# LayerNorm rows in PSUM, alternating half products and a fifth operand slot in a Strassen-type MLP

## The chip, the core and the metric

One core of a Trainium2 chip runs the whole kernel. The metric is the device time in microseconds, the median of several executions. The engines: PE (TensorE, matrix products into PSUM), DVE (VectorE), ACT (ScalarE), POOL (GpSimd), SP (SyncE, which issues most transfers). [...]

## The reference

A layer on 1024 tokens and 16 meta tokens, width 1024, fp32: LayerNorm, an input projection, three mixers (stick-breaking attention, a convolution module, a short gated convolution), an output projection, LayerNorm, an MLP and a last LayerNorm. The change touches the MLP's second product and the last LayerNorm:

```python
h = layer_norm(DEEPNORM_ALPHA * h + mix, ln_mix_g, ln_mix_b)
ff = jnp.square(jax.nn.relu(h @ w1)) @ w2       # 1024 -> 4096 -> 1024
h = layer_norm(DEEPNORM_ALPHA * h + ff, ln_ff_g, ln_ff_b)
return h[:, N_META:]
```

## The kernel before

Every fp32 matrix is split in a high part, rounded to the type that PE multiplies fast (`split`: ACT casts, DVE subtracts), and a low part; a product is three matmuls, high by high, high by low, low by high. The sum of all rows (1024 tokens x 1024 columns, eight row tiles of 128 tokens) stays in SBUF as `acc`.

The MLP runs in `NG` = 8 groups of 512 hidden columns (`ff_group`). First, four 128-column pieces of h @ w1 are formed for two halves of the tokens each (`ff1_chunk`); ACT applies relu out of PSUM, DVE squares into `ra`. Then the group's part of the second product is formed not by eight half products but by seven, of sums and differences of the quarters (a11 to a22 of the squares, b11 to b22 of w2), in the manner of Strassen and Winograd. The sums stand in `gsum` and run on POOL; `early_sums(1)` and the line behind it (L908 and L909) stand behind the last chunk of the first product. A `product` is, for each of four token tiles, 2 x 3 matmuls of 128x128 by 128x512 into one PSUM bank each; `add_to` adds the four banks to `acc` on DVE, and in the last group also writes each row's sum.

The operands of a half product are split by `a_part` (ACT casts, DVE forms the low part) and `b_part` (ACT casts, POOL forms the low part). Their parts lie in a ring of 4 slots of 8 KB per partition (L821): two for the product that runs, two for the next. PSUM has four banks with tag `g` for the products, three `t` and one `o` that are no longer used in the groups.

The scale and the offset of the last LayerNorm, `fg` and `fb`, are broadcast to SBUF before the groups (L960 to L963). In the last group `finish_rows` runs for a row tile as soon as its sums are complete, for tiles 0 to 3 after the fifth product, for tiles 4 to 7 after the last: the mean on POOL, the squares' sum on ACT (L870), the factor on POOL (L89, L91, L872), normalising on ACT (L873), scale on DVE (L874), offset on POOL, for the last tile on DVE (L876), output by SP (L877).

The order on each queue is set by a planner, which takes the program's order as priority and starts what it reckons to be ready; on the chip each engine then runs its queue in that fixed order. Waits for tiles and slots are put in by the same layer.

Of the kernel before, what the change touches and what calls it, by code (L numbers as in the profile page):

```python
# [8 lines left out]
F32 = mybir.dt.float32  # L9
F32R = mybir.dt.float32r  # L10
AF = mybir.ActivationFunctionType
ALU = mybir.AluOpType
# [3 lines left out]
P = 128  # L16
D = 1024
# [4 lines left out]
NT = S // P  # L22
# [13 lines left out]
def f32(ap):  # L36
    return ap.bitcast(F32)
# [3 lines left out]
def hybrid_layer(ctx: ExitStack, tc, x, meta_tokens, ln_in_g, ln_in_b, w_in, w_conf_dw, b_conf_dw,  # L41
                 ln_conf_g, ln_conf_b, w_short_dw, g_mix, w_out, ln_mix_g, ln_mix_b, w_ff1, w_ff2,
                 ln_ff_g, ln_ff_b, out):
    nc = tc.nc
    xs, os_ = x[0], out[0]
# [18 lines left out]
    def ps_t(shape):  # L64
        return ps.tile(shape, F32, tag="t", bufs=3, name="ps_t")

    def ps_o(shape):
        return ps.tile(shape, F32, tag="o", bufs=1, name="ps_o")
# [9 lines left out]
    first = cst.tile([P, 1], F32, name="first")  # L78
# [5 lines left out]
    def small(shape, name, bufs=4):  # L84
        return cst.tile(shape, F32, tag=name, bufs=bufs, name=name)

    def rsqrt(dst, src, n, w, scale, eps):
        ve = small([P, 8], "ve")
        nc.gpsimd.tensor_scalar(out=ve[:n, :w], in0=src, scalar1=scale, scalar2=eps,  # L89
                                op0=ALU.mult, op1=ALU.add)  # L90
        nc.gpsimd.tensor_tensor(out=dst, in0=ve[:n, :w], in1=mhalf[:n, :w], op=ALU.pow)  # L91
# [33 lines left out]
    def split(h, l, src):  # L125
        nc.scalar.copy(out=h, in_=src)  # L126
        nc.vector.tensor_tensor(out=l, in0=src, in1=f32(h), op=ALU.subtract)  # L127
# [5 lines left out]
    def raw_tile(name="raw"):  # L133
        return wA.tile([P, D], F32, tag="raw", bufs=2, name=name)
# [19 lines left out]
    def bcast_row(dst, row, eng=nc.scalar):  # L154
        eng.dma_start(out=dst, in_=row.partition_broadcast(P))
# [5 lines left out]
    rows = ph0.tile([P, 2, D], F32, name="rows")  # L161
# [628 lines left out]
    HALF = slice(0, 512), slice(512, 1024)  # L790
# [15 lines left out]
    def ff1_open(g, j):  # L806
        if j % 2 == 0:
            ra[j // 2] = wA.tile([P, 2, S], F32, tag="ff", bufs=2, name="relu2")
        u = 4 * g + (j + 2) % 4
        return halves(load_cols(w_ff1, u * P))  # L810

    def ff1(g, j):
        w = ff1_open(g, j)
        for c in range(2):
            ff1_chunk(j, w, c)

    def gsum(dst, a, b, op):
        nc.gpsimd.tensor_tensor(out=dst, in0=a, in1=b, op=op)  # L818

    def ring(name):  # L820
        return ffp.tile([P, 2, 2, 512], F32R, tag="ring", bufs=4, name=name)  # L821

    def a_part(src):
        hl = ring("a_hl")
        split(hl[:, 0], hl[:, 1], src)
        return hl

    def b_part(src):
        hl = ring("b_hl")
        nc.scalar.copy(out=hl[:, 0], in_=src)  # L830
        gsum(hl[:, 1], src, f32(hl[:, 0]), ALU.subtract)
        return hl

    def w2_load(g):

        rb = [ffp.tile([P, 2, D], F32, tag=f"w2_{h}", bufs=1, name=f"w2_{h}") for h in range(2)]
        for h in (1, 0):
            r0 = (4 * g + 2 * (1 - h)) * P
            nc.sync.dma_start(out=rb[h], in_=w_ff2[r0:r0 + 2 * P, :].rearrange("(u p) c -> p u c", p=P))
        return rb  # L840

    def product(a, b, banks, start):
        for tt in range(4):
            i = 0
            for u in range(2):
                for x, y in ((0, 0), (0, 1), (1, 0)):
                    nc.tensor.matmul(banks[tt], lhsT=a[:, x, u, tt * P:(tt + 1) * P], rhs=b[:, y, u, :],  # L847
                                     start=(start and i == 0), stop=(i == 5), skip_group_check=True)
                    i += 1

    def add_to(th, n, banks, first, sums=None):
        for tt in range(4):
            t = 4 * th + tt
            a = acc[:, t, HALF[n]]
            kw = {} if sums is None else dict(accum_out=sums[t][:, n:n + 1])
            if first:
                nc.vector.scalar_tensor_tensor(out=a, in0=a, scalar=ALPHA, in1=banks[tt], op0=ALU.mult, op1=ALU.add)
            elif sums is None:
                nc.vector.tensor_tensor(out=a, in0=banks[tt], in1=a, op=ALU.add)  # L859
            else:  # L860
                nc.vector.scalar_tensor_tensor(out=a, in0=banks[tt], scalar=1.0, in1=a, op0=ALU.mult, op1=ALU.add, **kw)

    def finish_rows(t, sm):

        a = acc[:, t, :]
        mv, rs = small([P, 2], "mv"), small([P, 2], "rs")
        nc.gpsimd.tensor_tensor(out=mv[:, 0:1], in0=sm[:, 0:1], in1=sm[:, 1:2], op=ALU.add)  # L867
        nc.gpsimd.tensor_scalar(out=mv[:, 1:2], in0=mv[:, 0:1], scalar1=-1.0 / D, scalar2=0.0, op0=ALU.mult, op1=ALU.add)  # L868
        junk = raw_tile("junk")
        nc.scalar.activation(out=junk, in_=a, func=AF.Square, bias=mv[:, 1:2], accum_out=sm[:, 2:3])  # L870
        rsqrt(rs[:, 0:1], sm[:, 2:3], P, 1, 1.0 / D, LN_EPS)
        nc.gpsimd.tensor_tensor(out=rs[:, 1:2], in0=rs[:, 0:1], in1=mv[:, 1:2], op=ALU.mult)  # L872
        nc.scalar.activation(out=a, in_=a, func=AF.Identity, scale=rs[:, 0:1], bias=rs[:, 1:2])  # L873
        nc.vector.tensor_tensor(out=a, in0=a, in1=fg, op=ALU.mult)  # L874
        eng = nc.vector if t == NT - 1 else nc.gpsimd
        eng.tensor_tensor(out=a, in0=a, in1=fb, op=ALU.add)  # L876
        nc.sync.dma_start(out=os_[t * P:(t + 1) * P, :], in_=a)  # L877

    def ff_group(g, opened=()):
        first, last = g == 0, g == NG - 1  # L880
        sums = {t: ffp.tile([P, 4], F32, tag="sums", bufs=NT, name="sums") for t in range(NT)} if last else None
        rb = w2_load(g)
        b11, b12 = (rb[0][:, :, h] for h in HALF)
        b21, b22 = (rb[1][:, :, h] for h in HALF)
        t1 = ffp.tile([P, 2, 512], F32, tag="t1", bufs=1, name="t1")
        gsum(t1, b12, b11, ALU.subtract)
        gsum(b12, b22, b12, ALU.subtract)
        for j in (2, 3, 0):
            if j not in opened:
                ff1(g, j)  # L890
        a11, a21 = (ra[0][:, :, h] for h in HALF)
        a12, a22 = (ra[1][:, :, h] for h in HALF)
        s1 = ffp.tile([P, 2, 512], F32, tag="s1", bufs=1, name="s1")

        def early_sums(u):
            gsum(s1[:, u], a21[:, u], a22[:, u], ALU.add)
            gsum(a21[:, u], a11[:, u], a21[:, u], ALU.subtract)

        early_sums(0)
        w = ff1_open(g, 1)  # L900
        ff1_chunk(1, w, 0)
        b, a = b_part(b21), a_part(a12)
        b_, a_ = b_part(b11), a_part(a11)
        gsum(b11, b22, t1, ALU.subtract)
        gsum(b21, b21, b11, ALU.subtract)
        gsum(a11[:, 0], s1[:, 0], a11[:, 0], ALU.subtract)
        ff1_chunk(1, w, 1)
        early_sums(1)  # L908
        gsum(a11[:, 1], s1[:, 1], a11[:, 1], ALU.subtract)  # L909

        def banks():
            return [ps_g([P, 512]) for _ in range(4)]

        pc = banks()
        product(a, b, pc, True)
        add_to(0, 0, pc, first)
        pa = banks()
        product(a_, b_, pa, True)
        add_to(0, 0, pa, False, sums)
        a, b = a_part(a11), b_part(b11)  # L920
        gsum(a12, a12, a11, ALU.subtract)
        product(a, b, pa, False)
        add_to(1, 0, pa, first)
        a, b = a_part(s1), b_part(t1)
        product(a, b, pa, False)
        add_to(1, 1, pa, first)
        a, b = a_part(a12), b_part(b22)
        product(a, b, pa, False)
        add_to(0, 1, pa, first, sums)
        if last:  # L930
            for t in range(4):
                finish_rows(t, sums[t])
        a, b = a_part(a21), b_part(b12)
        pb = banks()
        product(a, b, pb, True)
        add_to(1, 1, pb, False, sums)
        a, b = a_part(a22), b_part(b21)
        product(a, b, pb, False)
        add_to(1, 0, pb, False, sums)
        if last:  # L940
            for t in range(4, NT):
                finish_rows(t, sums[t])

    w0 = v_slot()
    raw = raw_tile()
# [1 line left out]
                      in_=w_ff1[:, 0:P].rearrange("(k p) c -> p k c", p=P))  # L947
# [9 lines left out]
    for pl in (attw, attq, keep):  # L957
        pl.release()
    ffp = pool("ffp", side="left")
    fg = ffp.tile([P, D], F32, name="fg")  # L960
    fb = ffp.tile([P, D], F32, name="fb")
    bcast_row(fg, ln_ff_g[0])
    bcast_row(fb, ln_ff_b[0])  # L963
    ff1_chunk(3, w1, 0)
    for g in range(NG):
        ff_group(g, (2, 3) if g == 0 else ())
# [28 lines left out]
```

## Time and profile before

| | |
|---|---|
| median of 3 runs | 1292.7 us (1291.52 to 1293.79) |
| profiled execution | 1289.94 us |
| its span in the trace | 1288.2 us |
| mean granted clock of PE | 0.968 |
| busy: PE, DVE, ACT, POOL | 1188.9, 861.4, 481.7, 432.5 us |
| last matmul starts | 1253.35 us |

The profile is that of one execution. A row of a timeline has the start in us from the span's start, the duration, the engine, the line of the kernel, the operation and its tiles, out<-in; in brackets the idle time of the engine before it and what ended it. PEld is PE's weight load. In tables of groups, the busy time is in us and the mean of one instruction in ns. Names of tiles are those of the program: `relu`, `s`, `w`, `t` are the operands ra, s1, w2 and t1.

### The profile page before, as it was taken

The numbers are of one execution on the slowest core, as the hardware profiler recorded it, in microseconds if no ns is written. First come the engines' busy times: TensorE is split into PE (matmuls) and PEld (weight loads), VectorE is DVE, ScalarE is ACT, GpSimd is POOL, SyncE is SP. The second block draws the span as 40 slices with busy tenths as digits, with TensorE's granted clock in tenths as the row PEclk, the third lists the DMA queues.
The fourth block names the chain that finished last, engine by engine and source line by source line (L and its number), as shares of the span: only waits on it lengthen the run. The fifth ranks groups of instructions, "written<-read, shape, count | busy, mean of one in ns | idle before, by whom it ended". The sixth has DMA issues, their size and how long they took to land. (4 is left out here: it accounts for less than half of the span.)

```text
span 1288.2 us, 15800 instructions
## 1 busy us (share of the span) xinstructions
PE 1188.9 (92%) x6126; PEld 1021.0 (79%) x6126; DVE 861.4 (67%) x1133; ACT 481.7 (37%) x883; POOL 432.5 (34%) x382
## 2 busy tenths in 40 slices
PE   5999996899899798989999999999999999999990
PEld 5999995889698687868778788887887878878870
DVE  6799967988787799674663645745447365463474
ACT  5422116667565554342322322322223222232243
POOL 3300002010100000240853634635436455353567
PEclk9999997999999899999999999999999999999995
DMA  9213211021201712103211111211211111111003
GB/s 296 108 50 82 65 35 50 17 50 34 50 18 41 221 34 66 50 17 109 72 66 33 33 66 49 64 35 49 66 50 46 53 49 66 37 30 66 1 2 129
DMA packets 71322, 78.97 MB, mean 61 GB/s; under 512 B 2329, under 2 KB 57920, under 8 KB 71248
## 3 DMA queue, kind: packets, MB, share of 16 engines
q1 hardware_dynamic: 66880, 67.18, 16.5%
q0 software_dynamic: 2304, 4.20, 1.7%
q10 hardware_dynamic: 2064, 6.59, 1.4%
q8 instruction: 48, 0.79, 0.3%
q14 instruction: 26, 0.21, 0.1%
HBM read 63.28 MB, written 10.49 MB: 57 GB/s over the span
## 5 line engine op out<-in xcount | busy, mean ns | idle before, releaser
L847 PE MATMUL ps_g<-b_hl,a_hl 128*128 128x512 f32 x1344 | 312.1, 392 | 6.3 <-POOL b_hl L818 3.8
L799 PE MATMUL ps_g<-x1h,w_hl 128*128 128x512 f32 x992 | 307.3, 389 | 0.0
L847 PEld LDWEIGHTS ps_g<-b_hl,a_hl 128*128 128x128 f32 x1344 | 252.6, 189 | 64.4 <-POOL b_hl L818 6.7
L208 PE MATMUL ps_g<-xh,w_hl 128*128 128x346 f32 (+4 forms) x1024 | 257.7, 331 | 0.9 <-ACT beta L458 0.9
L799 PEld LDWEIGHTS ps_g<-x1h,w_hl 128*128 128x128 f32 x992 | 186.2, 188 | 38.4
L818 POOL TENSOR_TENSOR b_hl<-w,b_hl 128x1024 fp32r<-128x1024 f32 x48 | 125.7, 2618 | 221.8 <-ACT b_hl L830 221.8
L804 DVE TENSOR_TENSOR relu<-sq 128x512 f32<-128x512 f32 x64 | 64.6, 1009 | 193.8 <-ACT sq L803 193.8
L799 PE MATMUL ps_g<-x1l,w_hl 128*128 128x512 f32 x496 | 193.0, 389 | 0.0
L208 PEld LDWEIGHTS ps_g<-xh,w_hl 128*128 128x128 f32 x1024 | 179.0, 191 | 9.9 <-ACT beta L458 1.1
L859 DVE TENSOR_TENSOR acc<-ps_g,acc 128x512 f32<-128x512 f32 x192 | 128.6, 686 | 65.0 <-PE ps_g L847 65.0
L208 PE MATMUL ps_g<-xl,w_hl 128*128 128x346 f32 (+4 forms) x512 | 169.4, 331 | 0.7 <-DVE xl L127 0.7
L803 ACT ACTIVATE sq<-ps_g 128x512 f32<-128x512 f32 x64 | 38.3, 598 | 248.7 <-PE ps_g L799 243.1
L799 PEld LDWEIGHTS ps_g<-x1l,w_hl 128*128 128x128 f32 x496 | 93.1, 188 | 19.4
L127 DVE TENSOR_TENSOR w_hl<-raw,w_hl 128x1024 fp32r<-128x1024 f32 x59 | 99.5, 1687 | 13.1 <-ACT w_hl L126 13.0
L126 ACT CAST a_hl<-relu 128x1024 fp32r<-128x1024 f32 x48 | 50.6, 1054 | 144.6 <-PE ps_g L847 59.7
L208 PEld LDWEIGHTS ps_g<-xl,w_hl 128*128 128x128 f32 x512 | 97.5, 191 | 5.0 <-DVE xl L127 1.0
L461 DVE TENSOR_TENSOR_SCAN keepp<-keepp 128x912 f32<-128x912 f32 (+7 forms) x64 | 87.6, 1380 | 10.4 <-ACT keepp L457 9.9
L127 DVE TENSOR_TENSOR a_hl<-relu,a_hl 128x1024 fp32r<-128x1024 f32 x48 | 68.8, 1433 | 29.2 <-ACT a_hl L126 29.2
L126 ACT CAST w_hl<-raw 128x1024 fp32r<-128x1024 f32 x59 | 61.8, 1047 | 62.2 <-PE ps_g L208 31.7
L283 DVE SCALAR_TENSOR_TENSOR cacc<-glu,prm,cacc 128x482 f32<-128x482 f32 (+3 forms) x120 | 82.7, 744 | 0.3
L830 ACT CAST b_hl<-w 128x1024 fp32r<-128x1024 f32 x48 | 50.3, 1048 | 54.9 <-DMA w<-in_w_ff_dram 54.6
L453 PE MATMUL ps_g<-ks,q_hl 128*128 128x456 f32 (+8 forms) x224 | 58.6, 365 | 9.0 <-ACT beta L458 3.9
(190 smaller groups left out, 1626.0 us busy)
## 6 DMA issues: line engine op xcount, KB each, us to landing
raw<-in_w_ff_dram SPq DMA_DIRECT2D x32, 512.0 KB, 4.1
w<-in_w_ff_dram SPq DMA_DIRECT2D x16, 1024.0 KB, 5.0
raw<-in_w_in_dram SPq DMA_DIRECT2D x22, 512.0 KB, 4.5
xt<-in_x_dram SPq DMA_DIRECT2D x8, 512.0 KB, 5.5
h_scr<-ht ACTq DMA_DIRECT2D x8, 512.0 KB, 2.9
q_hl<-q_hl POOLq DMA_DIRECT2D x16, 256.0 KB, 3.0
raw<-in_w_out_dram SPq DMA_DIRECT2D x8, 512.0 KB, 3.5
acc<-h_scr SPq DMA_DIRECT2D x8, 512.0 KB, 7.5
```

Of the source, the lines that this page charges most:

```text
L126: nc.scalar.copy(out=h, in_=src)
L127: nc.vector.tensor_tensor(out=l, in0=src, in1=f32(h), op=ALU.subtract)
L208: nc.tensor.matmul(dst[:, :cw], lhsT=w[:, a, k, :], rhs=b[:, k, c0:c0 + cw], start=(i == 0), stop=(i == 3 * KT - 1))
L283: nc.vector.scalar_tensor_tensor(out=acc, in0=glu[j][:, o + k:o + k + n], scalar=prm[:, j, k:k + 1], in1=acc, op0=ALU.mult, op1=ALU.add)
L453: nc.tensor.matmul(zp[:, :cm], lhsT=qs[h][:, m, i * P:(i + 1) * P], rhs=ks[:, h, c0:c0 + cm], start=(m == 0), stop=(m == 1 and not last))
L461: nc.vector.tensor_tensor_scan(out=rev, data0=rev, data1=rev, initial=1.0, op0=ALU.mult, op1=ALU.bypass)
L799: nc.tensor.matmul(pg, lhsT=w[a][:, k, :], rhs=b[:, k, c * 512:(c + 1) * 512], start=(i == 0), stop=(i == 3 * KT - 1))
L804: nc.vector.tensor_tensor(out=ra[j // 2][:, j % 2, HALF[c]], in0=sq, in1=sq, op=ALU.mult)
L818: nc.gpsimd.tensor_tensor(out=dst, in0=a, in1=b, op=op)
L830: nc.scalar.copy(out=hl[:, 0], in_=src)
L847: nc.tensor.matmul(banks[tt], lhsT=a[:, x, u, tt * P:(tt + 1) * P], rhs=b[:, y, u, :], start=(start and i == 0), stop=(i == 5), skip_group ...
L859: nc.vector.tensor_tensor(out=a, in0=banks[tt], in1=a, op=ALU.add)
```

## The change

The ring gets a fifth slot, `b_part` stands in front of `a_part` at each product, and three of POOL's sums per group (L908, L909) go to DVE. `fg` and `fb` are no longer loaded before the groups. In the last group, `ln_ff_rows` loads the two rows into the buffers of t1 and s1 by SP, and ACT copies each, in two halves, to the four PSUM banks that were unused. `finish_rows` reads them from there: for tiles 0 to 4 DVE scales in two halves and POOL adds the offset from SBUF as before; for tiles 5 to 7 DVE does all of it, (a - mean) * scale into a ring slot y and then y * factor + offset, in two halves each, and ACT no longer normalises. The last tile's halves go out by SP and by ACT. The last two half products of the last group are taken token tile by token tile in the order 0, 1 of the first, 0 of the second, 2, 1, 3, 2, 3, each followed by its addition, and by `finish_rows` where the tile is complete.

```diff
     def ring(name):
-        return ffp.tile([P, 2, 2, 512], F32R, tag="ring", bufs=4, name=name)
+        return ffp.tile([P, 2, 2, 512], F32R, tag="ring", bufs=5, name=name)
...
-    def product(a, b, banks, start):
-        for tt in range(4):
+    def product(a, b, banks, start, tts=range(4)):
+        for tt in tts:
...
+    def ln_ff_rows():
+        rows, banks = [], []
+        for tag, row in (("t1", ln_ff_g), ("s1", ln_ff_b)):
+            r = ffp.tile([P, D], F32, tag=tag, bufs=1, name="ln_ff")
+            bcast_row(r, row[0], nc.sync)
+            rows.append(r)
+        for i in range(4):
+            bk = ps_t([P, 512]) if i < 3 else ps_o([P, 512])
+            nc.scalar.copy(out=bk, in_=rows[i // 2][:, HALF[i % 2]])
+            banks.append(bk)
+        return rows[1], banks[:2], banks[2:]
...
-        nc.gpsimd.tensor_tensor(out=rs[:, 1:2], in0=rs[:, 0:1], in1=mv[:, 1:2], op=ALU.mult)
-        nc.scalar.activation(out=a, in_=a, func=AF.Identity, scale=rs[:, 0:1], bias=rs[:, 1:2])
-        nc.vector.tensor_tensor(out=a, in0=a, in1=fg, op=ALU.mult)
-        eng = nc.vector if t == NT - 1 else nc.gpsimd
-        eng.tensor_tensor(out=a, in0=a, in1=fb, op=ALU.add)
-        nc.sync.dma_start(out=os_[t * P:(t + 1) * P, :], in_=a)
+        rows = slice(t * P, (t + 1) * P)
+        if t < 5:
+            nc.gpsimd.tensor_tensor(out=rs[:, 1:2], in0=rs[:, 0:1], in1=mv[:, 1:2], op=ALU.mult)
+            nc.scalar.activation(out=a, in_=a, func=AF.Identity, scale=rs[:, 0:1], bias=rs[:, 1:2])
+            for n in range(2):
+                nc.vector.tensor_tensor(out=a[:, HALF[n]], in0=gps[n], in1=a[:, HALF[n]], op=ALU.mult)
+            nc.gpsimd.tensor_tensor(out=a, in0=a, in1=fb, op=ALU.add)
+            nc.sync.dma_start(out=os_[rows, :], in_=a)
+            return
+        y = ring("y").bitcast(F32)[:, 0].rearrange("p u c -> p (u c)")
+        for n in range(2):
+            nc.vector.scalar_tensor_tensor(out=y[:, HALF[n]], in0=a[:, HALF[n]], scalar=mv[:, 1:2], in1=gps[n],
+                                           op0=ALU.add, op1=ALU.mult)
+        for n in range(2):
+            nc.vector.scalar_tensor_tensor(out=a[:, HALF[n]], in0=y[:, HALF[n]], scalar=rs[:, 0:1], in1=bps[n],
+                                           op0=ALU.mult, op1=ALU.add)
+            if t == NT - 1:
+                (nc.sync, nc.scalar)[n].dma_start(out=os_[rows, HALF[n]], in_=a[:, HALF[n]])
+        if t < NT - 1:
+            nc.sync.dma_start(out=os_[rows, :], in_=a)
...
-        early_sums(1)
-        gsum(a11[:, 1], s1[:, 1], a11[:, 1], ALU.subtract)
+        early_sums(1, nc.vector)
+        nc.vector.tensor_tensor(out=a11[:, 1], in0=s1[:, 1], in1=a11[:, 1], op=ALU.subtract)
...
-        a, b = a_part(a11), b_part(b11)
+        b, a = b_part(b11), a_part(a11)
...
+        if last:
+            ln = ln_ff_rows()
+        b, a = b_part(b22), a_part(a12)
         product(a, b, pa, False)
         add_to(0, 1, pa, first, sums)
...
+        b_, a_ = b_part(b21), a_part(a22)
+        for step in (0, 1, 4, 2, 5, 3, 6, 7):
+            tt = step % 4
+            if step < 4:
+                product(a, b, pb, True, (tt,))
+                add_to(1, 1, pb, False, sums, (tt,))
+            else:
+                product(a_, b_, pb, False, (tt,))
+                add_to(1, 0, pb, False, sums, (tt,))
+                finish_rows(4 + tt, sums[4 + tt], *ln)
...
-    fg = ffp.tile([P, D], F32, name="fg")
-    fb = ffp.tile([P, D], F32, name="fb")
-    bcast_row(fg, ln_ff_g[0])
-    bcast_row(fb, ln_ff_b[0])
```

## Rows read from the trace of the kernel before

**Rows 1.** Busy us of each engine over the span, with instructions, from the page.
```profile
PE 1188.9 (92%) x6126; PEld 1021.0 (79%) x6126; DVE 861.4 (67%) x1133; ACT 481.7 (37%) x883; POOL 432.5 (34%) x382
```

**Rows 2.** Busy us by stretch (PE, PEld, DVE, ACT, POOL), granted clock, DMA share, GB/s.
```profile
640.00:1200.00 560.00, 553.94 (x2421) 454.71 (x2420) 299.68 (x318) 153.79 (x176) 272.50 (x121) 1.00 0.16 50
...
1200.00:1253.80 53.80, 53.52 (x234) 43.23 (x232) 31.16 (x53) 20.92 (x25) 31.20 (x32) 1.00 0.00 0
...
1253.80:1288.20 34.40, 0.00 (x0) 0.00 (x0) 17.87 (x11) 10.63 (x13) 25.49 (x28) 0.56 0.31 122
```

**Rows 3.** Waits of PE, 640 to 1256 us: total us, times, longest.
```profile
PE ps_g L847 <- POOL b_hl L818: 3.8, 7, 0.6
```

**Rows 4.** Timeline, MLP: start, us, engine, line, operation; idle before.
```profile
1193.62 2.40 POOL L818 TENSOR_TENSOR w<-w,t 128x1024 f32<-128x1024 f32 x1
...
1193.70 2.86 DVE L804 TENSOR_TENSOR relu<-sq 128x512 f32<-128x512 f32 x1 [2.41 <-ACT sq L803]
...
1214.57 39.17 PE L847 MATMUL ps_g<-b_hl,a_hl 128*128 128x512 f32 x168
...
1216.13 0.69 DVE L859 TENSOR_TENSOR acc<-ps_g,acc 128x512 f32<-128x512 f32 x1
...
1218.97 1.29 POOL L818 TENSOR_TENSOR relu<-s,relu 128x512 f32<-128x512 f32 x1
...
1222.71 3.38 POOL L818 TENSOR_TENSOR b_hl<-w,b_hl 128x1024 fp32r<-128x1024 f32 x1
...
1231.28 1.05 ACT L126 CAST a_hl<-relu 128x1024 fp32r<-128x1024 f32 x1 [3.63 <-issue]
...
1232.37 1.23 DVE L127 TENSOR_TENSOR a_hl<-relu,a_hl 128x1024 fp32r<-128x1024 f32 x1 [0.44 <-ACT a_hl L126]
```

**Rows 5.** End of the chain of waits: start us, us, what.
```profile
1274.58 3.36 DVE acc L874
...
1277.97 3.25 DVE acc L876
```

**Rows 6.** Timeline of the tail, as in rows 4.
```profile
1238.91 0.68 DVE L861 SCALAR_TENSOR_TENSOR acc<-ps_g,acc 128x512 f32<-128x512 f32 x1
...
1239.52 0.69 DVE L861 SCALAR_TENSOR_TENSOR acc<-ps_g,acc 128x512 f32<-128x512 f32 x1
...
1250.99 1.24 DVE L874 TENSOR_TENSOR acc<-acc,fg 128x1024 f32<-128x1024 f32 x1
...
1252.62 2.35 POOL L876 TENSOR_TENSOR acc<-acc,fb 128x1024 f32<-128x1024 f32 x1
...
1252.76 3.29 DVE L874 TENSOR_TENSOR acc<-acc,fg 128x1024 f32<-128x1024 f32 x1
...
1254.93 1.17 POOL L872 TENSOR_TENSOR rs<-rs,mv 128x1 f32<-128x1 f32 x1
...
1255.98 0.68 DVE L861 SCALAR_TENSOR_TENSOR acc<-ps_g,acc 128x512 f32<-128x512 f32 x1
...
1281.24 1.64 SPq L877 DMA_DIRECT2D out_dram<-acc  x3
```

**Rows 7.** Groups by form, whole span: count, busy us, mean ns, idle before.
```profile
L857 DVE SCALAR_TENSOR_TENSOR acc<-acc,ps_g 128x512 f32<-128x512 f32 x16 | 10.6, 682 | 5.9 <-PE ps_g L847 5.9
...
L317 ACT COPY cyt<-ps_o 128x512 f32<-128x512 f32 x4 | 2.3, 580 | 1.6 <-issue 1.3 <-PE ps_o L315 0.3
```

**Rows 8.** Groups by form, 1238 to 1289 us.
```profile
L870 ACT ACTIVATE junk<-acc,mv 128x1024 f32<-128x1024 f32 x8 | 9.2, 1145 | 8.7 <-POOL mv L868 8.7
...
L91 POOL TENSOR_TENSOR rs<-ve,mhalf 128x1 f32<-128x1 f32 x8 | 5.2, 656 | 0.4
...
L868 POOL TENSOR_SCALAR mv<-mv 128x1 f32<-128x1 f32 x8 | 1.4, 191 | 0.2
```

**Rows 9.** DMA issues of the whole span: count, KB each, us to landing.
```profile
out_dram<-acc SPq DMA_DIRECT2D x8, 512.0 KB, 2.6
...
fg<-in_ln_ff_g_dram ACTq DMA_DIRECT2D x1, 512.0 KB, 4.0
```

More of the change, by code (lines that the diff above doesn't have):

```diff
@@ L849, in product, with add_to @@
                     i += 1
-    def add_to(th, n, banks, first, sums=None):
-        for tt in range(4):
+    def add_to(th, n, banks, first, sums=None, tts=range(4)):
+        for tt in tts:
             t = 4 * th + tt
@@ L861, in add_to, with finish_rows @@
                 nc.vector.scalar_tensor_tensor(out=a, in0=banks[tt], scalar=1.0, in1=a, op0=ALU.mult, op1=ALU.add, **kw)
-    def finish_rows(t, sm):
+    def ln_ff_rows():
[9 more added lines that the diff above has]
+        return rows[1], banks[:2], banks[2:]
+    def finish_rows(t, sm, fb, gps, bps):
         a = acc[:, t, :]
@@ L893, in ff_group, with early_sums @@
         s1 = ffp.tile([P, 2, 512], F32, tag="s1", bufs=1, name="s1")
[L895 to L899, printed above, removed]
+        def early_sums(u, eng):
+            eng.tensor_tensor(out=s1[:, u], in0=a21[:, u], in1=a22[:, u], op=ALU.add)
+            eng.tensor_tensor(out=a21[:, u], in0=a11[:, u], in1=a21[:, u], op=ALU.subtract)
+        early_sums(0, nc.gpsimd)
         w = ff1_open(g, 1)
@@ L923, in ff_group @@
         add_to(1, 0, pa, first)
-        a, b = a_part(s1), b_part(t1)
+        b, a = b_part(t1), a_part(s1)
         product(a, b, pa, False)
         add_to(1, 1, pa, first)
-        a, b = a_part(a12), b_part(b22)
+        if last:
+            ln = ln_ff_rows()
+        b, a = b_part(b22), a_part(a12)
         product(a, b, pa, False)
@@ L931, in ff_group @@
             for t in range(4):
-                finish_rows(t, sums[t])
-        a, b = a_part(a21), b_part(b12)
+                finish_rows(t, sums[t], *ln)
+        b, a = b_part(b12), a_part(a21)
         pb = banks()
[L935 to L942, printed above, removed]
+        if not last:
+            product(a, b, pb, True)
+            add_to(1, 1, pb, False)
+            b, a = b_part(b21), a_part(a22)
+            product(a, b, pb, False)
+            add_to(1, 0, pb, False)
+            return
+        b_, a_ = b_part(b21), a_part(a22)
[8 more added lines that the diff above has]
+                finish_rows(4 + tt, sums[4 + tt], *ln)
     w0 = v_slot()
```

## The prediction

> **What bounds the kernel now.** I read the page's busy times first: PE is 92% busy, no other engine above 79%, and that is PE's own weight load [rows 1]. The busy times by stretch part the span: from 640 to 1200 us, in the MLP's groups, PE is busy 553.94 of 560 us; from 1200 to 1253.8 it is busy 53.52 of 53.8; from there to the end at 1288.2 it does nothing [rows 2]. So there are two things to win around the change: 6.3 us of holes in the MLP, and a tail of 34.4 us. PE's waits give the holes their names: 3.8 us, in 7 waits of 0.6 us at most, are for POOL's low half of a right operand [rows 3]; the other 2.5 us are single waits. The last group's timeline shows the pattern: a11's sums end on POOL at 1220.26, and POOL's low half of b11 runs 3.38 us, to 1226.09, while the matmuls that need it are due at about 1225.8 [rows 4].
>
> The tail is read from the chain of waits: it ends in DVE's scale of the last row tile, 3.36 us, and its offset, 3.25 us [rows 5]. In the timeline the same scale takes 1.24 us at 1250.99, but 3.29 us at 1252.76, beside a POOL offset of 2.35 us, and a POOL instruction on one column takes 1.17 us there [rows 6] where another takes 0.19 us [rows 8]. So DVE instructions with both inputs in SBUF and POOL's adds hold each other up. At the end three output transfers are issued together, from 1281.24 us on, right behind the last DVE instruction [rows 6]; from there 7.0 us pass to the end of the span.
>
> **The change part by part.** *Holes in the MLP.* In each group three 128x512 sums leave POOL (1.29 us each) for DVE, behind the last square; b operands are split before a operands; and with a fifth slot a b operand can be split a product earlier than its a. The seven products of a group take 39.17 us, 5.6 us each [rows 4], so product 2 begins at 1220.2 and product 3, the one that waits, at 1225.8. After: three sums of 0.69 us from 1216.1 end near 1218.2; product 2's slot for a comes free at 1220.2; cast 1.05 us and low half 1.23 us [rows 4] end near 1222.6, 3.2 us early. b11 is summed well before, and with the free slot it can be split during the chunk in front. So the 3.8 us go, and the 0.28 us of the last group. Of the remaining 2.2 us I take 0.4, since an earlier split takes some other waits along. Sum: 4.5 us saved, bounds 0 and 6.3. What is queued behind the sums are DVE's additions, which free the banks for product 2: the first ended at 1216.82, product 2 begins at 1220.2, 3.4 us in hand; the sums take 2.1 of it. Nothing is lost as long as DVE runs them at 0.69 us.
>
> *The rows in PSUM.* Before, both rows were loaded once, ahead of the groups, beside other work. Now SP issues two 512 KB broadcasts in the last group, into the buffers of t1 and s1, whose splits end near 1226 and 1228; nothing stands behind them on SP but the outputs, from 1255 on. One such load took 4.0 us [rows 9], so both lie near 1235. Four ACT copies of 128x512 write them to PSUM. No row has that direction; the nearest, out of PSUM, takes 0.58 us [rows 7]. Bounds 0.3 and 1.2 us each; I take the row's, 2.3 us for the four. ACT stood idle 3.6 us before its cast at 1231.28 [rows 4], and the rows are first used near 1240. I take nothing; if a copy waits for its transfer in front of a cast, up to 2 us of PE.
>
> *Alternating products.* The matmuls are the same 48. Count from t5, the end of the product in front, 11.2 us before E, the end of the last matmul; a token tile of one product is 1.4 us. Tiles 4 to 7 have their sums at t5 + 5.0, 7.8, 10.6 and 12.0 where they had them at 7.8, 9.2, 10.6 and 12.0: only tiles 4 and 5 come earlier. New wait: the third step needs the last two operands at t5 + 2.8, not t5 + 5.6. The slot of the last a comes free at t5, cast and low half take 2.3 us, and squares of 1.15 us [rows 8] stand in ACT's queue. Behind that matmul all of PE's work is queued. Bounds 0 and 2.3 us; I take 0.7. So E moves by -4.5 + 0.7, from 1253.7 to 1249.9.
>
> *The tail.* From t5 on DVE has 8 additions, one low half, 10 halves of scale (tiles 0 to 4) and 12 halves (tiles 5 to 7). A half with one input in PSUM takes 0.68 us, PSUM as second input included [rows 7]; two of them start 0.61 us apart [rows 6]. They keep 0.68 us beside POOL, as the addition at 1255.98 did [rows 6]. 30 x 0.61 + 1.2 = 19.5 us. POOL has five adds of 2.35 us and for each tile four small instructions, three of 0.19 and a power of 0.66 us [rows 8], a fifth for tiles 0 to 4: 11.8 + 8 x 1.23 + 5 x 0.19 = 22.6 us. Neither is full from t5 on, and some 2 us of POOL's lie before it. The bare latency of tile 7 is E + 0.8 (addition) + 0.5 (mean) + 1.33 (square and its read-out; y is made beside it) + 0.9 (POOL) + 1.3 (two halves), E + 4.8. The loads ask for more: DVE ends at t5 + 19.5 = E + 8.3 at the earliest, POOL near t5 + 22 = E + 11 if tile 7 comes last there. I take E + 10 for the last instruction. Behind it a transfer of 2.6 us [rows 9] and 1.4 us of issue and end (an estimate: the 7.0 us before are 4.4 us more than one landing, and I give a third of that to each of the two further transfers). So the tail is 14 us instead of 34.5; bounds 9 and 22.
>
> [...]
>
> *Sum.* 1288.2 - 3.8 - 34.5 + 14 = 1263.9 us of span, 24.3 less. The profiled execution took 1289.94 us, 1.7 above its span, so 1265.6 on its scale. The median of the runs shown is 1292.7, 2.8 above the profiled execution; on that scale it is 1268.
>
> **The rivals.**
> 1. *The queues keep the tail long.* POOL's adds, and SP's order of transfers, stand in front of tile 7's instructions. For it: the three transfers held back before [rows 6]. Against: tiles 5 to 7 add nothing on POOL now. Price: two visits of tile 7 to POOL behind one add each, after POOL's other load: E + 11 + 3.6 = E + 14.6, and 7 us of transfers as before, E + 21.6: 1271.5 of span, time 1276.
> 2. *The contention stays.* If a row in PSUM does not free DVE of POOL, the 22 new halves take half of 3.29 us, 1.65 each: 36.3 + 8 x 0.61 + 1.2 = 42.4 us from t5, E + 31.2, with the transfer E + 35.2; time 1290. Against it: DVE's additions at 0.68 us beside POOL.
> 3. *Slower: the sums on DVE stop PE.* In every group they stand in front of the additions. Each has two SBUF inputs, and beside a POOL instruction of 2.40 us such a one took 2.86 us [rows 4]. Three, 8.6 us against 3.4 in hand, stop PE 5.2 us in each of 8 groups: +42, less the 24.3: time 1310. It decides from 3.0 us of stop per group on, that is from 2.1 us per sum. Against: with b11 split early, POOL has little to do at that place.
>
> **How the numbers follow.** Forecast 0.76 (its own range 1260 to 1275), rival 1 0.13, rival 2 0.04, rival 3 0.07. A measurement here can tell 0.2%, 2.6 us, from no change; rival 2 lies about there. So faster 0.89, same 0.04, slower 0.07. The range of 1258 to 1280 takes in a tail of 9 us (1263, and with all holes gone 1261, less scatter) at one end and rival 1 with late operands at the other; rivals 2 and 3 are left out.
>
> **What would show it.** Right: hardly a PE wait for POOL's low half; the scale's halves at 0.6 to 0.75 us; the last DVE instruction 8 to 12 us after the last matmul, the end 11 to 18 us after it. Wrong: scale halves near 1.6 us; PE waiting at product 2 for DVE's additions in every group; a hole of over 2.3 us in the alternating products; several transfers issued together at the end.

## The result and the profile after

The changed kernel takes 1270.78 us, median of 4 runs (1266.96 to 1273.01), against 1292.11 before (4 runs): ratio 0.9831, 95% interval 0.9803 to 0.9859. Its profiled execution took 1273.01 us with a span of 1271.2; forecast were 1268 us, within 1258 to 1280. The time lies 2.8 us from the forecast, but in part by luck: two errors partly cancel. The MLP gave 5.8 us more than was counted, the tail 10.1 us less.

Busy us by stretch (PE, PEld, DVE, ACT, POOL, then granted clock, DMA share, GB/s), changed kernel; rows 2 has those of before, whose last matmul ended 6.7 us later (the MLP is 9.6 us shorter, but began 2.9 us later in this execution):

```profile
640.00:1200.00 560.00, 557.75 (x2459) 461.17 (x2458) 319.63 (x345) 153.56 (x176) 246.83 (x103) 1.00 0.16 50
1200.00:1247.10 47.10, 47.09 (x208) 38.66 (x206) 32.89 (x57) 23.07 (x29) 28.45 (x32) 1.00 0.07 23
1247.10:1271.20 24.10, 0.00 (x0) 0.00 (x0) 11.70 (x21) 6.53 (x10) 12.86 (x20) 0.58 0.44 174
```

The tail without a matmul is 24.1 us instead of 34.5, and PE has no holes left in the last group. All waits of PE from 610 us on (total us, times, longest):

```profile
PE ps_g L847 <- DVE acc L857: 1.7, 1, 1.7
PE ps_g L847 <- DVE a_hl L127: 0.6, 1, 0.6
```

Both lie in the first group; the seven waits for POOL's low half [rows 3] are gone. The last group's timeline shows why (start, us, engine, line, operation, idle before):

```profile
1205.92 1.05 ACT L830 CAST b_hl<-w 128x1024 fp32r<-128x1024 f32 x1
...
1207.05 2.48 POOL L818 TENSOR_TENSOR b_hl<-w,b_hl 128x1024 fp32r<-128x1024 f32 x1 [4.82 <-ACT b_hl L830]
...
1208.84 38.24 PE L847 MATMUL ps_g<-b_hl,a_hl 128*128 128x512 f32 x168
...
1211.85 0.68 DVE L923 TENSOR_TENSOR s<-relu,relu 128x512 f32<-128x512 f32 x1
1212.45 0.68 DVE L859 TENSOR_TENSOR acc<-ps_g,acc 128x512 f32<-128x512 f32 x1
...
1215.07 2.40 POOL L818 TENSOR_TENSOR relu<-relu,relu 128x1024 f32<-128x1024 f32 x1 [4.29 <-DVE relu L936]
...
1216.13 2.43 DVE L127 TENSOR_TENSOR a_hl<-relu,a_hl 128x1024 fp32r<-128x1024 f32 x1 [0.60 <-ACT a_hl L126]
```

b11's low half ends at 1209.53, just after the seven products begin; before, it ended 11.5 us behind that point [rows 4]. The three sums on DVE run at 0.68 us between the additions. The low half of a11, both of whose inputs lie in SBUF, still takes 2.43 us beside POOL's sum of a12 (1215.07), and ends 1.2 us before the third product begins. The products take 38.24 us where they took 39.17.

The tail's timeline, POOL, ACT and DVE, same columns:

```profile
1246.46 2.36 POOL L891 TENSOR_TENSOR acc<-acc,ln_ff 128x1024 f32<-128x1024 f32 x1
1248.78 0.20 POOL L880 TENSOR_TENSOR mv<-sums 128x1 f32<-128x1 f32 x1
...
1249.09 2.35 POOL L891 TENSOR_TENSOR acc<-acc,ln_ff 128x1024 f32<-128x1024 f32 x1
1251.40 0.34 POOL L880 TENSOR_TENSOR mv<-sums 128x1 f32<-128x1 f32 x2
...
1251.84 2.35 POOL L891 TENSOR_TENSOR acc<-acc,ln_ff 128x1024 f32<-128x1024 f32 x1
...
1254.55 0.34 POOL L881 TENSOR_SCALAR mv<-mv 128x1 f32<-128x1 f32 x2
...
1257.05 1.22 ACT L888 ACTIVATE acc<-acc,rs 128x1024 f32<-128x1024 f32 x1
...
1258.30 1.29 DVE L890 TENSOR_TENSOR acc<-ps_t,acc 128x512 f32<-128x512 f32 x2 [8.69 <-ACT acc L888]
1259.51 4.03 DVE L896 SCALAR_TENSOR_TENSOR y<-acc,mv,ps_t 128x512 f32<-128x512 f32 x6
```

Read it from below. DVE stands still for 8.69 us, until ACT has normalised tile 4; everything for tiles 5 to 7 is queued behind that scale. ACT is late because POOL's small instructions of tile 4 to 7 stand in one queue with the offsets of tiles 0 to 3: the sums of the last tile are written by 1248.4, its mean is formed at 1254.55, behind three adds, the first of which was already running. The factor of tile 4, which ACT needs, stands behind the same adds. This is rival 1 in its first half. The adds themselves are no longer drawn out: all five take 2.35 to 2.42 us.

Groups by form in the tail, 1234 to 1272 us (count, busy us, mean ns, idle before):

```profile
L890 DVE TENSOR_TENSOR acc<-ps_t,acc 128x512 f32<-128x512 f32 x10 | 6.4, 683 | 8.7 <-ACT acc L888 8.7
L896 DVE SCALAR_TENSOR_TENSOR y<-acc,mv,ps_t 128x512 f32<-128x512 f32 x6 | 4.0, 743 | 0.0
L891 POOL TENSOR_TENSOR acc<-acc,ln_ff 128x1024 f32<-128x1024 f32 x5 | 11.8, 2367 | 1.5 <-DVE acc L890 1.5
```

### The profile page after: what moved, and what is told of

The parts are those of the page before. It is cut to its first block, busy times and chain, and to the rows that moved or that the text cites. A ratio compares the mean times of both kernels' runs of the same rounds, so it can differ in the third digit from the quotient of the medians.

```text
span 1271.2 us, 15805 instructions
## 1 busy us (share of the span) xinstructions
PE 1188.3 (93%) x6126; PEld 1025.3 (81%) x6126; DVE 873.5 (69%) x1170; ACT 481.0 (38%) x884; POOL 387.5 (30%) x353
## 5 line engine op out<-in xcount | busy, mean ns | idle before, releaser
L847 PE MATMUL ps_g<-b_hl,a_hl 128*128 128x512 f32 x1344 | 306.6, 389 | 2.3 <-DVE acc L857 1.7
L847 PEld LDWEIGHTS ps_g<-b_hl,a_hl 128*128 128x128 f32 x1344 | 252.1, 188 | 55.4 <-DVE acc L857 2.1
L208 PE MATMUL ps_g<-xh,w_hl 128*128 128x346 f32 (+4 forms) x1024 | 260.8, 334 | 0.9 <-ACT beta L458 0.9
L804 DVE TENSOR_TENSOR relu<-sq 128x512 f32<-128x512 f32 x64 | 70.2, 1097 | 194.1 <-ACT sq L803 194.1
L208 PEld LDWEIGHTS ps_g<-xh,w_hl 128*128 128x128 f32 x1024 | 181.8, 194 | 9.8 <-ACT beta L458 1.1
L127 DVE TENSOR_TENSOR w_hl<-raw,w_hl 128x1024 fp32r<-128x1024 f32 x59 | 95.9, 1625 | 12.9 <-ACT w_hl L126 12.7
L461 DVE TENSOR_TENSOR_SCAN keepp<-keepp 128x912 f32<-128x912 f32 (+7 forms) x64 | 87.7, 1380 | 10.3 <-ACT keepp L457 9.7
L127 DVE TENSOR_TENSOR a_hl<-relu,a_hl 128x1024 fp32r<-128x1024 f32 x48 | 71.6, 1492 | 29.0 <-ACT a_hl L126 29.0
L628 PE MATMUL ps_g<-w_hl,y 128*128 128x512 f32 x240 | 64.8, 407 | 1.8 <-DVE w_hl L127 1.6
```

Of the source, the lines that this page charges most:

```text
L208: nc.tensor.matmul(dst[:, :cw], lhsT=w[:, a, k, :], rhs=b[:, k, c0:c0 + cw], start=(i == 0), stop=(i == 3 * KT - 1))
L461: nc.vector.tensor_tensor_scan(out=rev, data0=rev, data1=rev, initial=1.0, op0=ALU.mult, op1=ALU.bypass)
L628: nc.tensor.matmul(dst, lhsT=y[a][:, t * P:(t + 1) * P], rhs=w[b][:, n * 512:(n + 1) * 512], start=(i == 0), stop=(i == last))
L804: nc.vector.tensor_tensor(out=ra[j // 2][:, j % 2, HALF[c]], in0=sq, in1=sq, op=ALU.mult)
```

## The experiments

Totals of one program scatter here by several us, and the MLP's first half product, up to which these programs differ at most in the early load of two rows, began between 631.1 and 635.4 us. So each run is read by its stages: the MLP's length from the first half product to the end of the last matmul, and the tail from there to the end of the span. These scatter less: the nine profiles with the MLP's edits whole show 612.3 or 612.4 us, and the four that differ from the changed kernel in the MLP alone (e4 to e7) have tails of 23.8 to 24.7 us, with 24.1 in the changed kernel. The table gives both from the profile, with the time and the ratio to the kernel before on the same chip. e5 to e8 are one run each, on a chip where the one run of the kernel before took 1286.6 us; of them the stages are used, not the time.

| kernel | MLP us | tail us | last DVE, POOL instruction ends, us into the tail | time us | ratio |
|---|---|---|---|---|---|
| before | 621.9 | 34.5 | 27.5, 26.4 | 1292.1 | |
| changed | 612.3 | 24.1 | 20.4, 15.0 | 1270.8 | 0.9831 (0.9803 to 0.9859) |
| e1 rows in SBUF | 612.3 | 26.6 | 20.5, 23.0 | 1273.8 | 0.9865 (0.985 to 0.988) |
| e2 no alternation | 612.3 | 24.0 | 20.3, 14.9 | 1273.0 | 0.9855 (0.984 to 0.987) |
| e3 no offset on POOL | 612.3 | 15.9 | 12.2, 6.2 | 1263.3 | 0.9778 (0.9762 to 0.9795) |
| e4 MLP as before | 621.7 | 24.6 | 20.8, 15.4 | 1281.1 | 0.992 (0.9905 to 0.9935) |
| e5 four slots | 619.6 | 24.7 | 21.0, 15.6 | 1280.7 | |
| e6 sums on POOL | 612.8 | 24.6 | 20.9, 15.5 | 1270.6 | |
| e7 a before b | 621.0 | 23.8 | 20.1, 14.7 | 1281.5 | |
| e8 work shared as before | 612.3 | 24.2 | 18.3, 20.5 | 1269.4 | |
| e9 tile 4 on DVE | 612.3 | 19.7 | 15.6, 10.9 | 1268.6 | 0.982 (0.9805 to 0.9834) |
| e10 two adds last | 612.3 | 20.0 | 13.1, 12.3 | 1267.8 | 0.981 (0.9793 to 0.9826) |
| e11 two offsets on DVE | 612.4 | 19.8 | 15.5, 7.5 | 1267.8 | 0.9811 (0.9797 to 0.9826) |
| e12 outputs earlier | 612.3 | 18.8 | 13.1, 12.3 | 1267.5 | 0.9807 (0.9792 to 0.9821) |

**e1, the rows read from SBUF.**

```diff
-        for i in range(4):
-            bk = ps_t([P, 512]) if i < 3 else ps_o([P, 512])
-            nc.scalar.copy(out=bk, in_=rows[i // 2][:, HALF[i % 2]])
-            banks.append(bk)
+        banks = [rows[i // 2][:, HALF[i % 2]] for i in range(4)]
```

> The changed kernel, but the last LayerNorm's scale and offset are read from SBUF (the late-loaded tiles), not from PSUM; halves, alternation, ring and sums stay. Theory A (the PSUM rows end the contention of DVE and POOL): the scale halves rise from 0.68 us to over 1 us beside POOL's adds, small POOL instructions go to 1.2 us, and the tail behind the last matmul grows from 24.1 us to 29 to 34. Rival B (the tail is set by POOL's adds in POOL's queue whatever DVE reads): tail 24 to 26 us, time within 2 us of the changed kernel.

The groups of the tail in e1, 1238 to 1290 us:

```profile
L887 DVE TENSOR_TENSOR acc<-ln_ff,acc 128x512 f32<-128x512 f32 x10 | 11.6, 1199 | 0.0
L893 DVE SCALAR_TENSOR_TENSOR y<-acc,mv,ln_ff 128x512 f32<-128x512 f32 x6 | 6.2, 1090 | 0.3 <-POOL mv L878 0.2
...
L91 POOL TENSOR_TENSOR rs<-ve,mhalf 128x1 f32<-128x1 f32 x7 | 5.5, 783 | 0.5
```

The contention is back: scale halves of 1.20 us for 0.68, y halves of 1.09 for 0.74. POOL's power takes 0.78 us for 0.55. So the mechanism is theory A's, but the tail of 26.6 us lies between the two ranges: 2.5 us longer, not 5 to 10. DVE ends as in the changed kernel (20.5 us into the tail), since the drawn-out halves take the place of its wait of 8.7 us. But the planner also put tile 4's scale behind tiles 5 to 7 on DVE, and tile 4's offset on POOL, which follows it and ends 23.0 us into the tail, is the last instruction here, so the 2.5 us are not a price of the contention alone:

```profile
1263.90 1.29 DVE L887 TENSOR_TENSOR acc<-ln_ff,acc 128x512 f32<-128x512 f32 x2
...
1265.33 2.34 POOL L888 TENSOR_TENSOR acc<-acc,ln_ff 128x1024 f32<-128x1024 f32 x1 [2.80 <-DVE acc L887]
```

**e2, no alternation**: `for step in (0, 1, 2, 3, 4, 5, 6, 7)`.

> The changed kernel with the last two half products one after the other (0 1 2 3, then 0 1 2 3). Theory A (POOL's adds hold back the means of tiles 4 to 7, so the earlier sums are not used): tail 23 to 26 us, time the same within 1.5 us. Rival B (alternation brings tiles 4 and 5 forward and the tail with them): the tail 2 to 3 us longer.

Tail 24.0 for 24.1, and DVE waits 8.6 us for the same ACT instruction. Alternating the products moved nothing, neither as a gain nor as a hole in PE.

**e3, no offset on POOL** (the line with `nc.gpsimd.tensor_tensor(out=a, in0=a, in1=fb, op=ALU.add)` for tiles 0 to 4 is taken out).

> The changed kernel without POOL's addition of the offset for row tiles 0 to 4; that part of the computation is left out. Theory A (five adds of 2.35 us in POOL's queue stand in front of the means of tiles 4 to 7): the means come as the sums are ready, DVE's wait of 8.7 us goes, the last DVE instruction comes 9 to 12 us behind the last matmul and the tail is 12 to 15 us instead of 24.1. Rival B (DVE's own load of 30 halves sets the end): the tail stays at 20 us or more.

DVE's waits in e3, 1238 to 1290 us, for 8.7 us in the changed kernel:

```profile
DVE acc L890 <- ACT acc L888: 0.4, 1, 0.4
```

The tail falls by 8.2 us to 15.9, the last DVE instruction ends 12.2 us behind the last matmul. POOL's adds are what the forecast tail lacked; 0.9 us more than expected remain. This run takes the adds away and not only their place in the queue; e10 parts the two.

**e4, the MLP as before, the tail changed** (four slots, a before b, sums on POOL).

> The changed kernel with the MLP's part undone: four slots, a split before b, all sums on POOL; the last LayerNorm's part stays. Theory A (a late low half of b11 cost 1.0 us in each group, half of it as waiting and half as stretched matmuls): the first product of the last group begins 5 to 7 us later after the second group's than in the changed kernel (82.6 us per group against 81.6), time 6 to 10 us longer, tail as in the changed kernel or up to 3 us longer. Rival B (only the 0.55 us per group of PE waits counted): 3.5 to 4.5 us longer.

MLP 621.7 us for 612.3, time 10.4 us longer (just above theory A's range), and PE waits 3.8 us in 7 waits for POOL's low half, the row of before to the digit. So the MLP's edits are worth 9.4 us, of which 3.1 stand in PE's wait rows (5.4 us in all here, 2.3 in the changed kernel). Most of the rest is inside PE's busy time, which fell on the products' line from 312.1 us before to 306.6 at the same count of 1344. Matmuls of L847 in groups 2 to 7, min, median and max in ns, first before, then changed:

```profile
L847 PE MATMUL ps_g<-b_hl,a_hl x1008: 387/389/504, 718.8 to 1170.8; 128*128 128x512 f32 x168
```

```profile
L847 PE MATMUL ps_g<-b_hl,a_hl x1008: 389/389/389, 719.2 to 1165.1; 128*128 128x512 f32 x168
```

One wait of before, in the second group:

```profile
730.18 0.50 PE L847 MATMUL ps_g<-b_hl,a_hl 128*128 128x512 f32 x1
...
731.24 0.50 PE L847 MATMUL ps_g<-b_hl,a_hl 128*128 128x512 f32 x1 [0.56 <-POOL b_hl L818]
```

Where nothing is late, a matmul begins 0.23 us after the one in front (168 in 38.24 us) though it is drawn 0.39 us long: they overlap. Here the two begin 1.06 us apart. Of the 0.83 us lost, 0.56 are counted as a wait; the rest is hidden in the matmul in front, which is drawn 0.50 us long and overlaps nothing.

The first group of before lost time in another way. Busy us of the engines, columns as in rows 2:

```profile
643.00:647.00 4.00, 1.49 (x3) 0.56 (x3) 4.00 (x5) 2.23 (x3) 4.00 (x2) 0.99 0.00 2
647.00:650.00 3.00, 2.86 (x7) 2.28 (x8) 1.50 (x2) 0.00 (x0) 3.00 (x2) 0.50 0.00 0
```

PE ran only three matmuls in 4 us, and in the 3 us behind them the granted clock was 0.50. Seven matmuls began about 0.43 us apart for 0.23, some 1.4 us in all. In the first groups of e4 and e7 117 matmuls took 28.43 and 28.44 us, from 647.96 and 649.01 us on, where e5's 117 took 26.81 and e6's 116 took 26.59; the changed kernel's clock was 1.00 from 643 to 655 us.

**e5 to e7, one edit of the MLP undone each**: `bufs=4`; the three sums by `gsum`; `a, b = a_part(...), b_part(...)` at every product.

> The changed kernel with four slots in the ring. The length from the MLP's first half product to the last matmul's end was 621.9 us before, 612.3 us changed, 621.7 us with all three of the MLP's edits undone. Theory A (any one edit's absence is covered by the other two: b11's split then starts when product 1 ends, and cast and POOL's low half, 3.6 us, end within product 2): 612 to 614 us. Rival B (the slot carries the gain): 618 us or more, with PE waits for POOL's low half in every group.

> The changed kernel with the three late sums of each group on POOL again. Theory A (b11 is split ahead of them, so POOL's 3.9 us only delay a11, which still is split in time): length of the MLP from the first half product to the last matmul 612 to 614.5 us. Rival B (the sums carry the gain): 618 us or more.

> The changed kernel with the a operand split before the b operand. Theory A (the order is covered by the slot and the sums): length of the MLP 612 to 615 us. Rival B (the order carries the gain, since the fifth slot then goes to an a operand and POOL's long low half starts last): 618 us or more.

e5 and e7 fell to rival B: 619.6 and 621.0 us, with 5.0 us of PE waits for POOL's low half in 8 waits. e6 went with theory A: 612.8. From group to group it takes 82.53 and 82.52 us in e5 and e7, 81.60 in e6, with 82.62 in e4 and 81.60 in the changed kernel: the slot and the order are worth something only together. The 1.4 us between e5 and e7 stand in the slower matmuls of e7's first group. The sums bring almost nothing: 0.5 us, all in the first group. The timeline of e5's last group shows the cause:

```profile
1214.01 12.26 PE L847 MATMUL ps_g<-b_hl,a_hl 128*128 128x512 f32 x53
...
1219.71 1.05 ACT L830 CAST b_hl<-w 128x1024 fp32r<-128x1024 f32 x1 [4.84 <-PE ps_g L847]
1219.73 2.42 POOL L818 TENSOR_TENSOR relu<-relu,relu 128x1024 f32<-128x1024 f32 x1 [5.81 <-DVE relu L936]
...
1222.10 3.38 POOL L818 TENSOR_TENSOR b_hl<-w,b_hl 128x1024 fp32r<-128x1024 f32 x1
```

Without a free slot b11's cast waits for the end of product 1, and its low half comes behind a12's sum of 2.42 us in POOL's queue, which itself waited 5.8 us for DVE's sum of a11. With the slot and b first it begins before product 1 (1207.05 above). My expectation overlooked that sum, and so did the prediction, for it stood there before too:

```profile
1220.34 2.42 POOL L818 TENSOR_TENSOR relu<-relu,relu 128x1024 f32<-128x1024 f32 x1
```

In e7 the two stand in the same order on POOL: a12's sum at 1221.65, b11's low half at 1224.02.

**e8, the tail's work shared out as before, scale from PSUM** (`if t < 8`, offset on POOL, on DVE for tile 7).

> The changed kernel with the last LayerNorm's work shared out as before (ACT normalises, DVE scales, POOL adds the offset, DVE for the last tile, one output each), but with the scale read from PSUM, and with the MLP's edits and the alternation. It splits the tail's gain of 10.4 us: theory A (reading from PSUM gave 2.5 us of it, the rest comes from tiles 5 to 7 leaving ACT's and POOL's queues): tail 30 to 33 us. Rival B (the end of the contention gives most once POOL has seven adds): tail 24 to 27 us.

Tail 24.2 us: rival B. All of the tail's 10.3 us come already with the scale read from PSUM in halves (alternation and the MLP's edits give the tail nothing, by e2 and e4); giving tiles 5 to 7 to DVE adds nothing to it. With e1, which has the second without the first and a tail of 26.6, each of the two brings most of it alone. What reading in halves does by itself was not run. DVE waits 8.6 us for ACT here too, and its scale halves take 0.68 us.

**e9 to e12, on from the cause.** e9: `if t < 4`. e10: also the offsets of tiles 2 and 3 put behind tile 7's last small instruction on POOL (`with tc.issue_after(power)`). e11: e9, with these two offsets added by DVE from PSUM. e12: e10, with the y halves of tiles 6 and 7 put behind the output halves of tiles 4 and 5.

> The changed kernel with row tile 4 finished wholly on DVE like tiles 5 to 7; POOL adds the offset for tiles 0 to 3. Theory A (two things hold the end: POOL's adds in front of the means of tiles 5 to 7, and DVE's queue behind tile 4's scale, which waits for ACT; the second is gone): DVE's wait of 8.7 us shrinks to waits for the means, tail 17 to 21 us instead of 24.1, time 3 to 7 us shorter than the changed kernel. Rival B (POOL's adds alone set it): tail 23 to 25 us.

> The changed kernel with tile 4 on DVE and POOL's offset for tiles 2 and 3 put behind the last small instruction of tile 7 in POOL's queue; tiles 0 and 1 as before. Theory A (the adds' place in POOL's queue costs what the run without adds gave back, 8.2 us): the means of tiles 5 to 7 come as their sums are ready, the last DVE instruction 10 to 13 us behind the last matmul, POOL's last add 9 to 13 us behind it, tail 14 to 17 us, time 7 to 10 us shorter than the changed kernel. Rival B (the adds only move, and POOL ends as late): tail 20 us or more.

> The changed kernel with tile 4 on DVE and the offset of tiles 2 and 3 added by DVE in halves out of PSUM instead of by POOL. Theory A: POOL's queue is free as with the adds put last, but DVE has four more halves of 0.61 us: tail 15 to 18 us. Rival B (DVE's load is the bound now, and the four halves delay its additions that free the banks): tail 19 us or more, or a hole in the last products of over 1 us.

> The kernel with tile 4 on DVE and two of POOL's offsets put last, in which DVE is made to write tile 4's and tile 5's output halves before it forms y for tiles 6 and 7. Theory A (its end is now set by the six tiles whose transfers start late, some 1.3 us each at 400 GB/s, so that an earlier first transfer counts): DVE still ends 12 to 14 us behind the last matmul, but the first of the last outputs starts 2.5 to 3 us earlier, tail 17 to 18.5 us instead of 20.0, time 1 to 3 us shorter than with the adds put last. Rival B (DVE's end and the last transfers behind it set the end): tail 19.5 to 20.5 us, no difference in time.

e9 shortens the tail by 4.4 us, half of what the adds cost, by taking tile 4's scale away from the head of DVE's queue; its median time is 2.2 us shorter, less than the 3 to 7 expected. e10 brings DVE's last instruction from 15.6 to 13.1 us into the tail, close to theory A's 10 to 13, so the adds' place in the queue does hold DVE back. But the tail stays at 20.0, rival B's number: the outputs now end it. SP's transfers in e10, and the busy row of the stretch behind them (the last three columns are granted clock, DMA share and GB/s):

```profile
1245.64 2.96 SPq L893 DMA_DIRECT2D out_dram<-acc  x2
1255.62 0.33 SPq L909 DMA_DIRECT2D out_dram<-acc  x1
1256.45 0.33 SPq L893 DMA_DIRECT2D out_dram<-acc  x1
```

```profile
1257.00:1264.00 7.00, 0.00 (x0) 0.00 (x0) 2.54 (x4) 0.00 (x0) 1.74 (x1) 0.50 1.02 398
```

Six of eight tiles, 3.1 MB, leave only after 1255.6; at the 0.40 MB per us of that row they take 7.9 us. e11 left no hole in PE, but its tail of 19.8 is rival B's: DVE's four more halves end it at 15.5 us. e12 lets the first of the six go at 1252.23, 2.7 us earlier from the last matmul than in e10: tail 18.8, 1.2 us less, between the two ranges and nearer to theory A's 17 to 18.5. In time e10, e11 and e12 cannot be told apart, nor from the changed kernel by their intervals, so the 7 to 10 us expected of e10 are not there; by medians the three are 3 us faster than it, by the tail 4 to 5.

## Why the prediction was right, and where it was not

*Holes in the MLP: right wait, mis-sized.* Forecast 4.5 us less 0.7, measured 9.6. The term was read from PE's wait rows alone. A late operand costs 1.03 us a group (82.63 us from group to group before, 81.60 after, from the starts of the second and the last group's products), 0.55 as a wait and the rest in the matmuls beside it, which the profile counts as busy. The first group gave 2.5 us instead of 0.4, of which some 1.4 are its stretch of lower clock. Of the three edits I named, two carry it, and only together (e5, e7). What stood in front of b11's low half was a12's sum, which stayed on POOL, and not the three sums that went. The low half of a11 came 1.2 us early and not 3.2, since it took 2.43 us where I took 1.23.

*Rows in PSUM: right.* Loads issued at 1220.86 and 1222.27, ACT's copies (1.11 us for two, then 0.59 and 0.58) done by 1227.86, 14 us before DVE's first use at 1242.30; PE did not wait. (Before, the splits of s1 and t1 ended at 1227.95 and 1230.22, not near 1226 and 1228 as I read; nothing hung on it.)

*Alternating products: right in the price, wrong in the use.* No wait of PE came of it (0.7 taken, none seen), and no gain either (e2): the earlier sums of tiles 4 and 5 met a POOL queue with the offsets in front.

*The tail: the step that failed.* "I take E + 10 for the last instruction": it was E + 20.4. The halves cost nearly what was said, 0.68 and 0.74 us at 0.60 to 0.66 us from start to start, and transfer and end took 3.7 us for 4.0 forecast. The load of DVE alone, E + 8.3, was a lower bound that no run reached: without the adds, e3 ends it at E + 12.2. What failed was adding up loads as if queues had no order: the planner set three offsets of 2.35 us in front of tile 7's mean, and tile 4's scale in front of all of DVE's work for tiles 5 to 7. Rival 1 had this mechanism at E + 14.6 with 7 us of transfers; its sum of 21.6 was nearer to the measured 24.1 than my 14, with too little in the queues and too much in the transfers. Of the signs I named, PE's waits and the halves came as for right; the last instruction (8 to 12 us after the last matmul, measured 20.4) and the end (11 to 18, measured 24.1) did not.

*Rival 2* fell: the halves took 0.68 us beside POOL's adds. Where the rows lie in SBUF, e1 shows 1.20 us on average (the rival took 1.65). *Rival 3* fell in the last group, where the sums ran at 0.68 us with POOL idle beside them, and no group from the second on has a wait for DVE. But in the first group its mechanism shows once: a sum took 2.29 us with POOL busy (two instructions, 2.85 us from 637.13 and 1.73 us from 639.94 on), and PE waited for an addition queued behind it.

```profile
638.24 2.29 DVE L923 TENSOR_TENSOR s<-relu,relu 128x512 f32<-128x512 f32 x1
...
642.68 0.68 DVE L857 SCALAR_TENSOR_TENSOR acc<-acc,ps_g 128x512 f32<-128x512 f32 x1
...
643.41 4.85 PE L847 MATMUL ps_g<-b_hl,a_hl 128*128 128x512 f32 x20 [1.67 <-DVE acc L857]
```

Without the sums on DVE (e6) PE's first group has two other waits, of 2.5 us in all, so nothing is won by taking them back.

Why e3 ends DVE's work at E + 12.2 where the load alone asked for 8.3 shows in DVE's busy time (third figure) in the 11.2 us before the last matmul's end and from there on:

```profile
1236.50:1247.70 11.20, 11.20 (x50) 8.96 (x48) 9.21 (x21) 10.74 (x14) 6.70 (x24) 1.00 0.18 71
1247.70:1260.00 12.30, 0.02 (x1) 0.00 (x0) 11.84 (x21) 5.15 (x9) 3.76 (x13) 0.65 0.53 210
```

It is 21.1 us of work for the 19.5 of my sum, with 2.0 us idle before the last matmul's end and some 0.4 after it. What would have filled that idle time was not tried.

## What to carry to other kernels

Where an engine is shared by long filler work and the short steps of a critical chain, add up its queue in its order, not its load: three 2.35 us adds in front of a 0.2 us mean, and one scale in front of the twelve halves of tiles 5 to 7, go with 8.2 us of tail here (e3). A PE that is "99% busy" can still hide late operands, since matmuls that no longer overlap count as busy (in the second group of before one is drawn 0.50 us where 0.23 lie from start to start): compare the period of a repeated group with its matmul count times the bare distance between matmuls. And undo edits one at a time: of the six made here, two work only together, two (the rows in PSUM, tiles 5 to 7 on DVE) each bring most of the same gain, and two (the sums, the alternation) do next to nothing.

## What the runs showed of the hardware

In e1's tail DVE's halves of 128x512 values with two SBUF operands took 1.20 us (scale), 1.09 us (y) and 0.75 us (output) on average. With one of the operands in PSUM they took 0.68, 0.74 and 0.74 us in the changed kernel, and DVE's additions 0.68 us with it as the second ([rows 7], L857). ACT copied 128x512 from SBUF to PSUM in 0.58 to 0.59 us, as fast as the other way [rows 7]. Output transfers that overlap moved at 0.40 MB per us (398 GB/s from 1257 to 1264 us of e10). At that rate the 4.2 MB of result need 10.5 us (an estimate from that row), and the outputs became the end of the tail once the engines were ready in time. In the first group of before, PE's granted clock was 0.50 from 647 to 650 us; from 643 to 647 it had run three matmuls.
